# Turned heads written into the tiles of the output sums, a reordered output pair and later turns, in a two-layer hybrid encoder

## The chip, the cores and the metric

The kernel runs on one core of a Trainium2 chip. The core has TensorE (PE, matrix products), VectorE (DVE, elementwise), ScalarE (ACT, activations and casts), GpSimd (POOL, here small powers and the issue of DMAs) and SyncE (SP, here only the issue of DMAs). Each has its own queue of instructions, worked off in order; the transfers themselves run on DMA engines that all queues share. The metric is the device time of one execution in microseconds (us), as a median over runs; less is better.

## What is computed

Two layers of a streaming encoder on 512 tokens of width 2048, all in float32. One layer, cut to its core:

```python
h = rmsnorm(x, g_pre)
gq, gk, gv, gg, ga, aq, ak, av, ag = split_columns(h @ w_in)
log_a = log_sigmoid(ga @ w_alpha + b_alpha) / 16
o_gla = gla_chunk_causal(gq, gk, gv, log_a)        # 4 heads of 256 values
o_gla = rmsnorm(o_gla, g_gla) * silu(gg)
o_att = chunk_band_attention(aq, ak, av, rel_bias) # 8 heads of 128 values
o_att = rmsnorm(o_att, g_att) * silu(ag)
y = concatenate([o_gla, o_att]) @ w_out
x = x + rmsnorm(y, g_post)
```

What matters here is the end: the gated outputs of both head groups, concatenated to 2048 columns, are the left operand of the output projection.

## The kernel before

**Products.** A float32 value is split into a high part (a cast by ACT, L106 or L191) and a low part (a subtraction by DVE, L107 or L199), and a product takes three matmuls: high by high, high by low, low by high. Most products run in pairs of 512-column weight blocks by a scheme in the manner of Strassen (`fast_gemm`, L316): the operand is cut into token halves and halves of the 2048 rows, and seven products P1 to P7 of half size, on sums of operand quarters, take the place of eight. Each product runs over four chunks of 256 rows, so a pair is 28 jobs of 12 matmuls; "52" is P5 on the third chunk. The order of the 28 is written out: `PROD` (L132) for input pairs, `PROD_END` (L133) for output pairs. P1 and P2 and the last P4 use plain operands; P5, P6, P7 and P3 use the sums S1, S2, S3 and S4, which are made beforehand, written to DRAM and loaded again for each pair (`sa`). P2 of an output pair has accumulators of its own, two of the four auxiliary PSUM banks (L391). The weights' own sums are made by DVE as jobs come up (L185, L187).

**Jobs ahead.** `stream` (L206) lists all jobs in order. When a job has been issued, `ahead` (L240) issues the loads of weights (and of `sa`) up to five jobs ahead, casts up to four and low parts up to three. All these loads go through SP's queue, which is in order: a load that waits holds those behind it.

**Tasks and turns.** Side work is written as generators in the list `tasks`, and `pump` (L249) takes one step of the first of them; a `Pace` calls it after every job, three steps per job in the gate pair and the first output pair. Entries of `delayed` are run once they have been counted down by so many steps. The program so written is ordered once more per engine by a planner, which goes by modelled times and by when slots of tiles become free.

**The path into the output pair.** The last input pair is GG, the gate of the GLA heads (L1226). When one of its four results (P3, P7, P2, P4, in this order) is there, `gg_consume` (L1215) takes its SiLU (L1218) and multiplies two normalised heads by it (L1221). That gives two heads h for one token half p, 2 and 3 first, 0 and 1 with P2 and P4. Two and three steps later `turn_gla` (L1135) turns each: four transposes on PE (L1139), eviction with the gain by ACT (L1148) into `full_o`, a write of it to DRAM (`fg`, L1152, POOL's queue), and the split into the operand `og`. Chunk c of the output pair is GLA head c with attention heads 2c and 2c+1; the latter were turned during attention and lie in DRAM as `fa` (and, split, as `oa`). `output_sums` (L551) waits until both halves of head c are turned, loads the four quarters of the chunk from `fa` and `fg` into four tiles, and makes S1, S3, S2, S4 (L535 to L544), each split and written to DRAM (`oS`, L525, POOL's queue). The order of chunks is 2, 3, 0, 1.

**Tiles.** Tiles called `t2` come from a ring of eight; `full_o`, the SiLUs, the four quarters and many short results share it. Tiles named g0 to g17 are single slots reused in turn: in this part g9 and g10 have held GLA states and g12 and g13 the turned queries, and later the residual rows (L458, POOL's queue) come into g16, g17, g12, g13, g9 and g10. `residual_rows` (L1295) stands in the task list behind the sums.

After GG comes the first output pair, W01 (L1318), in both layers. In layer 0 the other half of the output follows as standard products (`std_gemm`), in layer 1 as a second fast pair, W23.

Of the kernel before, what the change touches and what calls it, by code (L numbers as in the profile page):

```python
# [8 lines left out]
F32R = mybir.dt.float32r  # L9
# [6 lines left out]
P = 128  # L16
L = 2
# [16 lines left out]
def hybrid_trunk(  # L34
# [34 lines left out]
    def slot(tag, shape, dtype=F32):  # L69
        return slots.tile([P] + shape, dtype, tag=tag, name=nm(tag))  # L70
# [4 lines left out]
    def t2(shape=(512,), dtype=F32):  # L75
        return tmp.tile([P] + list(shape), dtype, tag="t2", name=nm("t2"))
# [13 lines left out]
    def dram(shape, name):  # L90
        return dpool.tile(shape, F32, tag=name, name=name)
# [4 lines left out]
    so_d = [{(n, c): dram([P, 1024], f"o{n}{l}{c}") for n in ("S1", "S2", "S3", "S4") for c in range(4)} for l in range(L)]  # L96
    oa_d = [{(h, c): dram([P, 1024], f"oa{l}{h}{c}") for h in range(2) for c in range(4)} for l in range(L)]
    of_att = [[dram([P, 2, 512], f"fa{l}{c}") for c in range(4)] for l in range(L)]
    of_gla = [{(h, c): dram([P, 512], f"fg{l}{h}{c}") for h in range(2) for c in range(4)} for l in range(L)]
    fac_d = [dram([P, 1024], f"fac{l}") for l in range(L)]  # L100

    def flat(t):
# [26 lines left out]
    def order(text):  # L129
        return [("P" + z[0], int(z[1])) for z in text.split()]  # L130

    PROD = order("10 11 50 12 51 13 52 53 60 61 30 62 63 31 70 32 71 33 72 73 20 21 40 22 41 23 42 43")  # L132
    PROD_END = order("10 20 11 21 12 22 13 23 50 51 60 52 61 53 62 63 30 31 32 33 70 71 72 73 40 41 42 43")  # L133
    LEFT = {"P5": "S1", "P6": "S2", "P3": "S4", "P7": "S3", "P4": "A22"}
    last_cast = [None]

# [70 lines left out]
    for l in range(L):  # L207
        if l:
            stream += [Job(l, "std", c, AG0) for c in CO]
            stream += [Job(l, "std", c, AG0) for c in CO]  # L210
            stream += [Job(l, "std", c, AG1) for c in CO]
        else:
            stream += [Job(l, "std", c, b) for b in (AG0, AG1) for c in CO]
        for b0, b1 in PAIRS:
            pr = {}
            stream += [Job(l, k, c, b0, b1, pr) for k, c in PROD]
        for b0, b1 in (W01, W23) if l == L - 1 else (W01,):
            pr = {}
            stream += [Job(l, k, c, b0, b1, pr) for k, c in PROD_END]
        if l < L - 1:  # L220
            stream += [Job(l, "std", c, b) for half in range(2) for b in W23 for c in OL]

# [93 lines left out]
    def fast_gemm(l, pair, consume, rate=0.0, skip=0, feature_major=False, after=None, end=False, lag=0, ops=A):  # L316
# [5 lines left out]
        if end:  # L322
            target.update(P2="Z", P4="Y")
            starts.append("P4")
        prod = PROD_END if end else PROD
        pace = Pace(rate, skip)
        keep = {}

# [55 lines left out]
                                stop=(c == 3 and kk == 1 and m == 2), skip_group_check=True,  # L384
                            )

        if end:
            acc["Z"] = None
        for k, c in prod:
            if k == "P2" and end and c == 0:  # L390
                acc["Z"] = [aux(), aux()]  # L391
# [121 lines left out]
    def make_sums(dst, tags, parts, home={}, chunks=range(4)):  # L513
        stage = [0]

        def put(name, c, src):
            if (name, c) in home:
                op = A[name, c] = slot(home[name, c], [2, 512], F32R)
            else:
                tag = tags[stage[0] % len(tags)]  # L520
                op = rtile(tag, dtype=F32R) if tag == "H" else slot(tag, [2, 512], F32R)
                stage[0] += 1
            with tc.issue_after(last_cast[0]):
                split(op[:, 0, :], op[:, 1, :], src)
            nc.gpsimd.dma_start(dst[name, c], flat(op))  # L525
            written.add((id(dst), name, c))

        for c in chunks:
            got = parts(c)
            while got is None:  # L530
                yield
                got = parts(c)
            a11, a12, a21, a22 = got
            yield
            nc.vector.tensor_tensor(out=a22, in0=a21, in1=a22, op=ALU.subtract)  # L535
            put("S1", c, a22)
            yield
            nc.vector.tensor_tensor(out=a21, in0=a11, in1=a21, op=ALU.subtract)
            put("S3", c, a21)
            yield  # L540
            nc.vector.tensor_tensor(out=a22, in0=a22, in1=a11, op=ALU.subtract)
            put("S2", c, a22)
            yield
            nc.vector.tensor_tensor(out=a12, in0=a12, in1=a22, op=ALU.add)  # L544
            put("S4", c, a12)
            yield

    def token_sums(l):
        return make_sums(sa_d[l], STAGE, lambda c: (full[0, c][:, 0, :], full[0, c][:, 1, :], full[1, c][:, 0, :], full[1, c][:, 1, :]), HOME)

    def output_sums(l, chunks, ready, tags):  # L551
        def parts(c):
            if not ready(c):
                return None
            tiles = [t2() for _ in range(4)]
            for half in range(2):
                nc.sync.dma_start(
                    tiles[2 * half].rearrange("p (k n) -> p k n", k=2),
                    of_att[l][c][:, :, half * 256 : (half + 1) * 256],
                )  # L560
                nc.sync.dma_start(tiles[2 * half + 1], of_gla[l][half, c])
            return tiles

        return make_sums(so_d[l], tags, parts, chunks=chunks)

    def both(a, b):
        turn = 0
        live = [a, b]
        while live:
            turn += 1  # L570
            try:
                next(live[turn % len(live)])
                yield
            except StopIteration:
                live.remove(live[turn % len(live)])

    VT = ("g16", "g17", "g4", "g5", "g6", "g7", "g12", "g13")
    V, U = {}, {}
# [137 lines left out]
    def layer(l):  # L716
# [151 lines left out]
        class Head:  # L868
# [69 lines left out]
            def turn(self):  # L938
                c, kk = self.hd // 2, self.hd % 2
                if kk == 0:  # L940
                    turned[c] = [slot(tag, [2, 512], F32R) for tag in ("g16", "g17")]
                ps = aux()
                for t in range(NT):
                    nc.tensor.transpose(ps[:, t * P : (t + 1) * P], self.sg[:, t, :], ident)
                kt = 8 + self.hd
                f = t2()
                nc.scalar.activation(
                    f, ps, AF.Copy, scale=gcol[:, l * 2 * KT + KT + kt : l * 2 * KT + KT + kt + 1]
                )
                nc.gpsimd.dma_start(of_att[l][c][:, kk, :], f)  # L950
                ks = slice(kk * 256, (kk + 1) * 256)
                for half in range(2):
                    z = turned[c][half]
                    split(z[:, 0, ks], z[:, 1, ks], f[:, half * 256 : (half + 1) * 256])
                    if kk:
                        nc.gpsimd.dma_start(oa_d[l][half, c], flat(z))
# [96 lines left out]
        class Unit:  # L1053
# [63 lines left out]
            def evict(self):  # L1117
# [14 lines left out]
        OG = {(0, 2): "g14", (0, 3): "g15", (0, 0): "a120", (0, 1): "a121",  # L1132
              (1, 2): "g4", (1, 3): "g5", (1, 0): "g6", (1, 1): "g7"}

        def turn_gla(h, p):  # L1135
            ps = aux()
            for f in range(2):
                for tt in range(2):
                    nc.tensor.transpose(  # L1139
                        ps[:, f * 256 + tt * P : f * 256 + (tt + 1) * P],  # L1140
                        normed[h, p][:, tt, f * P : (f + 1) * P], ident,
                    )
            assert p or h >= 2 or ("P2", h) in passed
            op = slot(OG[p, h], [2, 512], F32R)
            full_o = t2()
            for f in range(2):
                kt = 2 * h + f
                nc.scalar.activation(  # L1148
                    full_o[:, f * 256 : (f + 1) * 256], ps[:, f * 256 : (f + 1) * 256], AF.Copy,
                    scale=gcol[:, l * 2 * KT + KT + kt : l * 2 * KT + KT + kt + 1],  # L1150
                )
            nc.gpsimd.dma_start(of_gla[l][p, h], full_o)  # L1152
            split(op[:, 0, :], op[:, 1, :], full_o)
            og[p, h] = op
            O[1, p, OC.index(h)] = op
# [41 lines left out]
                    op_att[0, i] = O[0, 0, OC.index(i)] = slot(f"a11{i}", [2, 512], F32R)  # L1197
                    nc.sync.dma_start(flat(op_att[0, i]), oa_d[l][0, i])

        def output_ready(c):  # L1200
            return 2 * c in heads_done and (0, c) in og and (1, c) in og

        def gv_consume(j, h, t, src, comb):
            if (j, h) not in gvh:
# [10 lines left out]
        def gg_consume(j, h, t, src, comb):  # L1215
            until(lambda: len(gla_done) == 4)
            sg = t2()
            nc.scalar.activation(sg, settled(src, comb), AF.Silu)  # L1218
            for i in range(2):
                dst = normed[2 * j + i, h][:, t, :]  # L1220
                nc.vector.tensor_tensor(out=dst, in0=dst, in1=sg[:, i * 256 : (i + 1) * 256], op=ALU.mult)  # L1221
                if t:
                    delayed.append([2 + i, lambda hd=2 * j + i: turn_gla(hd, h)])

        tasks.append(output_sums(l, OC, output_ready, ("g0", "g1", "g2", "g3")))
        fast_gemm(l, PAIRS[5], gg_consume, rate=3, after=fetch_operands)  # L1226
        A.clear()

# [64 lines left out]
        xs = []  # L1293

        def residual_rows():  # L1295
            while len(og) < 8:
                yield
            for half in range(2):
                xs.append(load_tokens(half, x_src, nc.gpsimd))
                yield  # L1300
# [89 lines left out]
```

## Time and profile before

| | |
|---|---|
| median of 3 runs | 1704.12 us (1702.9 to 1708.93) |
| the profiled execution | 1700.16 us, of which the span is 1698.4 |
| busy: PE, DVE, ACT, POOL | 1628.3, 1267.1, 912.5, 156.4 us |
| PE's mean granted clock | 0.982 of full speed |
| DMA | 461.85 MB, mean 272 GB/s |
| W01 of layer 0 | from 648.45 to 759.83 us |
| W01 of layer 1 | from 1495.31 to 1606.41 us |

Rows of a timeline have the start, the duration, the engine, the line, the operation and the tiles (out<-in); in brackets stands how long the engine was idle before it and what ended that. In these names mm and ax are PSUM banks, wh and wl the high and low parts of weights, sa a loaded sum, a and g operands in slots, t a t2 tile, bias and sg tiles that hold gated heads here. Rows of a stretch have its bounds, its length, each engine's busy time and instruction count, the granted clock, the busy share of the DMA engines and their rate. "PE mm L381 x336" is the chain's row for 336 matmuls in sequence. Rows with "SPq" or "POOLq" and KB are DMA issues of a stretch with their median time from issue to landing.

### The profile page before, as it was taken

The numbers are of one execution on the slowest core, as the hardware profiler recorded it, in microseconds if no ns is written. First come the engines' busy times: TensorE is split into PE (matmuls) and PEld (weight loads), VectorE is DVE, ScalarE is ACT, GpSimd is POOL, SyncE is SP. The second block draws the span as 40 slices with busy tenths as digits, with TensorE's granted clock in tenths as the row PEclk, the third lists the DMA queues.
The fourth block names the chain that finished last, engine by engine and source line by source line (L and its number), as shares of the span: only waits on it lengthen the run. The fifth ranks groups of instructions, "written<-read, shape, count | busy, mean of one in ns | idle before, by whom it ended". The sixth has DMA issues, their size and how long they took to land.

```text
span 1698.4 us, 24821 instructions
## 1 busy us (share of the span) xinstructions
PE 1628.3 (96%) x8986; PEld 1389.0 (82%) x8986; DVE 1267.1 (75%) x1647; ACT 912.5 (54%) x1502; POOL 156.4 (9%) x236
## 2 busy tenths in 40 slices
PE   9999999999999998599999999999999999975996
PEld 7888999998887776488888889999988877764884
DVE  5977777776778877685786667777767787786878
ACT  7554446566554555454774444465665555554552
POOL 0110000010100112100122000000101001121002
PEclk9999999999999998899999999999999999987998
DMA  8889695876868689896789486858668676998965
GB/s 339 270 332 320 215 311 173 306 252 211 275 234 290 223 311 345 298 338 209 239 288 400 153 324 207 306 179 307 237 225 282 230 290 205 330 333 310 357 220 201
DMA packets 141690, 461.85 MB, mean 272 GB/s; under 512 B 15412, under 2 KB 28084, under 8 KB 141568
## 3 DMA queue, kind: packets, MB, share of 16 engines
q1 hardware_dynamic: 120096, 384.97, 65.6%
q0 software_dynamic: 20896, 74.21, 11.5%
q8 instruction: 71, 1.16, 0.3%
q10 hardware_dynamic: 576, 1.08, 0.2%
q14 instruction: 51, 0.42, 0.1%
HBM read 392.29 MB, written 67.91 MB: 271 GB/s over the span
## 4 chain that ended last, share of the span: by engine, by line
PE 85%; DMA 6%; issue 5%; DVE 2%; POOL 1%; ACT 0%; SPq 0%; DVEq 0%; POOLq 0%; ACTq 0%
PE mm L381 42%; PE mm L371 18%; PE mm L302 15%; PE ax L919 2%; DMA oS<-g 1%; DMA sa<-oS 1%; DMA raw<-in_w_dram 1%; PE ax L1101 1%; PE ax L902 1%; PE ax L739 1%; PE ax L1073 1%; DVE wl L199 1%; DMA t<-fg 1%; PE ax L381 1%; DMA bias<-in_rel_dram 1%
## 5 line engine op out<-in xcount | busy, mean ns | idle before, releaser
L381 PE MATMUL mm<-wh,sa 128*128 128x512 f32 x1600 | 521.9, 397 | 35.9 <-DMA sa<-oS 21.0
L191 ACT CAST wh<-raw 128x1024 fp32r<-128x1024 f32 (+1 forms) x253 | 265.2, 1053 | 257.3 <-PE mm L381 81.6
L381 PEld LDWEIGHTS mm<-wh,sa 128*128 128x128 f32 x1600 | 302.2, 189 | 110.3 <-ACT g L106 31.2
L199 DVE TENSOR_TENSOR wl<-raw,wh 128x1024 fp32r<-128x1024 f32 (+1 forms) x253 | 307.5, 1219 | 113.3 <-PE mm L381 52.3
L191 ACT CAST wh<-H 128x1024 fp32r<-128x1024 f32 x240 | 251.6, 1051 | 224.3 <-PE mm L381 111.5
L199 DVE TENSOR_TENSOR wl<-H,wh 128x1024 fp32r<-128x1024 f32 x240 | 292.9, 1222 | 100.7 <-PE mm L381 44.4
L381 PE MATMUL mm<-wl,sa 128*128 128x512 f32 x800 | 314.9, 394 | 0.0
L371 PE MATMUL mm<-sa,wh 128*128 128x256 f32 x1280 | 236.5, 285 | 0.0
L381 PE MATMUL mm<-wh,a 128*128 128x512 f32 x608 | 200.9, 395 | 3.1 <-ACT wh L191 2.4
L371 PEld LDWEIGHTS mm<-sa,wh 128*128 128x128 f32 x1280 | 199.6, 192 | 0.1
L371 PE MATMUL mm<-sa,wl 128*128 128x256 f32 x640 | 181.6, 284 | 0.0
L381 PEld LDWEIGHTS mm<-wl,sa 128*128 128x128 f32 x800 | 151.4, 189 | 29.4
L185 DVE TENSOR_TENSOR H<-H,raw 128x1024 f32<-128x1024 f32 x132 | 160.6, 1220 | 11.1 <-DMA raw<-in_w_dram 9.8
L423 POOL TENSOR_TENSOR sm<-sm,mhalf 128x2 f32<-128x2 f32 (+2 forms) x42 | 57.7, 1375 | 851.1 <-DVE sm L929 449.0
L381 PEld LDWEIGHTS mm<-wh,a 128*128 128x128 f32 x608 | 113.2, 188 | 27.4 <-ACT wh L191 4.3
L381 PE MATMUL mm<-wl,a 128*128 128x512 f32 x304 | 119.9, 394 | 3.2 <-DVE wl L199 3.2
L371 PEld LDWEIGHTS mm<-sa,wl 128*128 128x128 f32 x640 | 122.6, 192 | 0.2
L187 DVE TENSOR_TENSOR raw<-H,raw 128x1024 f32<-128x1024 f32 x60 | 73.4, 1224 | 61.1 <-DMA raw<-in_w_dram 60.9
L371 PE MATMUL mm<-a,wh 128*128 128x256 f32 x512 | 95.1, 286 | 0.0
L302 PE MATMUL mm<-wh,a 128*128 128x512 f32 x288 | 91.8, 390 | 0.0
L333 ACT COPY ev<-mm 128x512 f32<-128x512 f32 x96 | 55.9, 583 | 58.0 <-PE mm L381 41.2
L302 PE MATMUL mm<-wh,g 128*128 128x512 f32 x240 | 82.0, 392 | 0.0
(229 smaller groups left out, 2381.8 us busy)
## 6 DMA issues: line engine op xcount, KB each, us to landing
raw<-in_w_dram SPq DMA_DIRECT2D x323, 512.0 KB, 4.9
sa<-S SPq DMA_DIRECT2D x184, 512.0 KB, 4.4
H<-in_w_dram SPq DMA_DIRECT2D x60, 512.0 KB, 5.4
sa<-A SPq DMA_DIRECT2D x48, 512.0 KB, 6.4
sa<-oS SPq DMA_DIRECT2D x48, 512.0 KB, 5.7
S<-g POOLq DMA_DIRECT2D x32, 512.0 KB, 9.3
oS<-g POOLq DMA_DIRECT2D x32, 512.0 KB, 6.5
oa<-g POOLq DMA_DIRECT2D x16, 512.0 KB, 6.9
```

The source lines that it names most:

```text
L185: nc.vector.tensor_tensor(out=h, in0=h, in1=r, op=ALU.add)
L187: nc.vector.tensor_tensor(out=r, in0=h, in1=r, op=ALU.subtract)
L191: last_cast[0] = nc.scalar.copy(self.wh[:, z, :], src[:, z, :]).ins
L199: nc.vector.tensor_tensor(out=self.wl[:, z, :], in0=self.src[:, z, :], in1=self.wh[:, z, :].bitcast(F32), op=ALU.subtract)
L302: nc.tensor.matmul(pss[o], a(part, kk, o) if callable(a) else a[:, part, t], rhs[:, kk, :], start=(i == 0 and kk == 0 and m == 0), stop=(i ...
L333: nc.scalar.copy(e, src[t])
L371: nc.tensor.matmul(dst, lhs[:, kk, f], a[:, part, tok], start=(fresh and kk == 0 and m == 0 and ft % 2 == 0), stop=(c == 3 and kk == 1 and ...
L381: nc.tensor.matmul(out_ps[t], a[:, part, tok], rhs[:, kk, :], start=(fresh and kk == 0 and m == 0), stop=(c == 3 and kk == 1 and m == 2), ...
L423: nc.gpsimd.tensor_tensor(out=out_r, in0=v, in1=mhalf[:, : v.shape[-1]], op=ALU.pow)
L739: nc.tensor.matmul(ps[0:96, half * 256 : (half + 1) * 256], wga[kt // 10][:, kt % 10, :], op[:, i, (kt % 2) * 256 : (kt % 2 + 1) * 256], s ...
L902: nc.tensor.transpose(ps[:, j * P : (j + 1) * P], self.prob[i][:, j * P : (j + 1) * P], ident)
L919: nc.tensor.matmul(o, self.pt[i][:, j * P : (j + 1) * P], av[hd // 4, j // 2][:, j % 2, (hd % 4) * P : (hd % 4 + 1) * P], start=(j == 0), ...
```

## The change

- The turned head no longer goes through DRAM. `turn_gla` evicts it into the tile that the sums read. These tiles are slots now, g9 and g10 for chunks 2 and 0, g12 and g13 for chunks 3 and 1, two quarters to a slot; they are taken at the first turn of a chunk, where the two loads of `fa` are issued too. `of_gla` and `output_sums` are gone; `make_sums` is called with the tiles.
- Turns wait 8 and 11 steps, not 2 and 3.
- W01 in both layers follows `PROD_OUT`: P2 of its last two chunks (those of heads 0 and 1) comes behind P6 of the first two, and P5 and P6 run chunk pair by chunk pair. The second output pair of layer 1 keeps `PROD_END`.
- In layer 1 the split of the second token half of the turned attention heads, which nothing reads there, is left out with its write.
- `residual_rows` has no guard of its own any more; `both`, which nothing called, and an assignment that had no use are gone.

```diff
@@ orders
     PROD_END = order("10 20 11 21 12 22 13 23 50 51 60 52 61 53 62 63 30 31 32 33 70 71 72 73 40 41 42 43")
+    PROD_OUT = order("10 20 11 21 12 13 50 51 60 61 22 23 52 53 62 63 30 31 32 33 70 71 72 73 40 41 42 43")
...
-        prod = PROD_END if end else PROD
+        prod = (PROD_OUT if b0 == NB_IN else PROD_END) if end else PROD
@@ sums
-    def output_sums(l, chunks, ready, tags):
-        def parts(c):
-            if not ready(c):
-                return None
-            tiles = [t2() for _ in range(4)]
-            for half in range(2):
-                nc.sync.dma_start(
-                    tiles[2 * half].rearrange("p (k n) -> p k n", k=2),
-                    of_att[l][c][:, :, half * 256 : (half + 1) * 256],
-                )
-                nc.sync.dma_start(tiles[2 * half + 1], of_gla[l][half, c])
-            return tiles
-
-        return make_sums(so_d[l], tags, parts, chunks=chunks)
@@ attention heads
-                    turned[c] = [slot(tag, [2, 512], F32R) for tag in ("g16", "g17")]
+                    turned[c] = [slot(tag, [2, 512], F32R) for tag in ("g16", "g17")[: 1 + (not last)]]
...
-                for half in range(2):
-                    z = turned[c][half]
+                for half, z in enumerate(turned[c]):
@@ layer
+        parts = {}
+
+        def out_parts(c):
+            if c not in parts:
+                halves = [slot(tag, [2, 512]) for tag in (("g9", "g10"), ("g12", "g13"))[c % 2]]
+                parts[c] = [halves[0][:, 0, :], halves[0][:, 1, :], halves[1][:, 0, :], halves[1][:, 1, :]]
+                for half in range(2):
+                    nc.sync.dma_start(
+                        parts[c][2 * half].rearrange("p (k n) -> p k n", k=2),
+                        of_att[l][c][:, :, half * 256 : (half + 1) * 256],
+                    )
+            return parts[c]
@@ turn_gla
-            full_o = t2()
+            full_o = out_parts(h)[2 * p + 1]
...
-            nc.gpsimd.dma_start(of_gla[l][p, h], full_o)
@@ readiness, steps, task
-        def output_ready(c):
-            return 2 * c in heads_done and (0, c) in og and (1, c) in og
+        def ready_parts(c):
+            return parts[c] if (0, c) in og and (1, c) in og else None
...
-                    delayed.append([2 + i, lambda hd=2 * j + i: turn_gla(hd, h)])
+                    delayed.append([8 + 3 * i, lambda hd=2 * j + i: turn_gla(hd, h)])
...
-        tasks.append(output_sums(l, OC, output_ready, ("g0", "g1", "g2", "g3")))
+        tasks.append(make_sums(so_d[l], ("g0", "g1", "g2", "g3"), ready_parts, chunks=OC))
@@ residual rows
         def residual_rows():
-            while len(og) < 8:
-                yield
             for half in range(2):
```

More of the change, by code (lines that the diff above doesn't have):

```diff
@@ L98, in hybrid_trunk @@
     of_att = [[dram([P, 2, 512], f"fa{l}{c}") for c in range(4)] for l in range(L)]
-    of_gla = [{(h, c): dram([P, 512], f"fg{l}{h}{c}") for h in range(2) for c in range(4)} for l in range(L)]
     fac_d = [dram([P, 1024], f"fac{l}") for l in range(L)]
@@ L218, in hybrid_trunk @@
             pr = {}
-            stream += [Job(l, k, c, b0, b1, pr) for k, c in PROD_END]
+            stream += [Job(l, k, c, b0, b1, pr) for k, c in (PROD_OUT if b0 == NB_IN else PROD_END)]
         if l < L - 1:
@@ L385, in matmuls @@
                             )
-        if end:
-            acc["Z"] = None
         for k, c in prod:
@@ L549, in token_sums @@
         return make_sums(sa_d[l], STAGE, lambda c: (full[0, c][:, 0, :], full[0, c][:, 1, :], full[1, c][:, 0, :], full[1, c][:, 1, :]), HOME)
-    def output_sums(l, chunks, ready, tags):
-        def parts(c):
-            if not ready(c):
-                return None
-            tiles = [t2() for _ in range(4)]
-            for half in range(2):
-                nc.sync.dma_start(
-                    tiles[2 * half].rearrange("p (k n) -> p k n", k=2),
-                    of_att[l][c][:, :, half * 256 : (half + 1) * 256],
-                )
-                nc.sync.dma_start(tiles[2 * half + 1], of_gla[l][half, c])
-            return tiles
-        return make_sums(so_d[l], tags, parts, chunks=chunks)
[L566 to L572, printed above, removed]
-                yield
-            except StopIteration:
-                live.remove(live[turn % len(live)])
     VT = ("g16", "g17", "g4", "g5", "g6", "g7", "g12", "g13")
@@ L1295, in residual_rows @@
         def residual_rows():
-            while len(og) < 8:
-                yield
             for half in range(2):
```

## The prediction

> **What bounds the kernel now.** I read the page first (shares, the chain), then a table of stretches, then the engines' timelines around the first output pair. The page says that TensorE is the bound:
>
> ```profile
> span 1698.4 us, 24821 instructions
> PE 1628.3 (96%) x8986; PEld 1389.0 (82%) x8986; DVE 1267.1 (75%) x1647; ACT 912.5 (54%) x1502; POOL 156.4 (9%) x236
> ...
> PE 85%; DMA 6%; issue 5%; DVE 2%; POOL 1%; ACT 0%; SPq 0%; DVEq 0%; POOLq 0%; ACTq 0%
> ```
>
> So only idle or slow PE time can be won, and the stretches say where it is. The rows are attention and the pairs after it in layer 0; the last eight products of the gate pair (GG); the first output pair (W01) of layers 0 and 1; and 30 us late in W01 of layer 1. The chain's row is a whole pair of 28 products that nothing disturbs.
>
> ```profile
> core 0: us, PE busy (x) PEld busy (x) DVE busy (x) ACT busy (x) POOL busy (x), PEclk, DMA share, GB/s
> 246.00:594.00 348.00, 347.53 (x2144) 302.60 (x2143) 265.16 (x397) 199.44 (x384) 28.01 (x30) 1.00 0.72 247
> 626.60:648.45 21.85, 21.85 (x104) 18.15 (x104) 16.77 (x22) 13.10 (x20) 3.18 (x6) 1.00 0.96 337
> 648.45:759.83 111.38, 85.08 (x355) 68.11 (x354) 85.65 (x103) 54.87 (x81) 12.96 (x25) 0.89 0.90 326
> 1495.31:1606.41 111.10, 85.26 (x357) 68.57 (x356) 86.25 (x103) 55.76 (x82) 12.96 (x25) 0.88 0.93 341
> 1580.00:1610.00 30.00, 30.00 (x134) 24.87 (x133) 26.10 (x29) 15.80 (x24) 0.00 (x0) 1.00 0.98 378
> ```
> ```profile
> 102.52 76.16 PE mm L381 x336
> ```
>
> A pair needs 76.2 us; W01 takes 111.4 and 111.1. Of the 35 us too much in each layer, 26 are idle (111.38 - 85.08), the rest a granted clock of 0.89. W01 begins at 648.45, where the left operand becomes a. PE's timeline shows two stalls per layer, at the same places:
>
> ```profile
> 648.45 0.39 PE L381 MATMUL mm<-wh,a 128*128 128x512 f32 x1
> ...
> 663.08 0.45 PE L1139 MATMUL ax<-cst,bias 128*128 128x128 f32 x1 [2.42 <-DVE bias L1221]
> 667.96 0.45 PE L1139 MATMUL ax<-cst,bias 128*128 128x128 f32 x1 [2.76 <-DVE bias L1221]
> 675.86 0.49 PE L1139 MATMUL ax<-cst,sg 128*128 128x128 f32 x3
> 709.36 0.77 PE L381 MATMUL mm<-wh,sa 128*128 128x512 f32 x1 [14.84 <-ACT g L106]
> 712.91 0.77 PE L381 MATMUL mm<-wh,sa 128*128 128x512 f32 x2
> 1509.81 0.45 PE L1139 MATMUL ax<-cst,bias 128*128 128x128 f32 x1 [2.44 <-DVE bias L1221]
> 1515.30 0.45 PE L1139 MATMUL ax<-cst,bias 128*128 128x128 f32 x1 [3.36 <-DVE bias L1221]
> 1555.04 0.77 PE L381 MATMUL mm<-wh,sa 128*128 128x512 f32 x1 [15.58 <-DMA sa<-oS]
> ```
>
> The first stall: turns stand ahead of P2 in PE's queue and wait for gated heads. The second: P5 of chunk 0 waits for S1. What made these late is in the queues of ACT, DVE and POOL and the chain:
>
> ```profile
> 637.56 0.81 PE L1139 MATMUL ax<-cst,g 128*128 128x128 f32 x6
> ```
> ```profile
> 642.53 0.69 DVE L338 TENSOR_TENSOR ev<-mm,ev 128x512 f32<-128x512 f32 x1 [1.04 <-PE mm L381]
> ...
> 654.29 0.68 DVE L535 TENSOR_TENSOR t<-t,t 128x512 f32<-128x512 f32 x1
> ```
> ```profile
> 646.89 0.82 ACT L1148 ACTIVATE t<-ax,gcol 128x256 f32<-128x256 f32 x2
> ...
> 660.30 1.15 ACT L1218 ACTIVATE t<-ev 128x512 f32<-128x512 f32 x2
> ...
> 666.54 0.62 ACT L1218 ACTIVATE t<-mm 128x512 f32<-128x512 f32 x1
> ...
> 692.86 0.83 ACT L1148 ACTIVATE t<-ax,gcol 128x256 f32<-128x256 f32 x2
> ```
> ```profile
> 670.20 0.43 DVE L1221 TENSOR_TENSOR sg<-sg,t 128x256 f32<-128x256 f32 x1
> ```
> ```profile
> 694.25 0.54 POOL L1152 DMA_DIRECT2D fg<-t  x1 [15.56 <-ACT t L1148]
> ```
> ```profile
> 648.79 5.09 DMA t<-fg
> ```
>
> Two turns' transposes are over by 638.4, but ACT evicts one of them only at 646.9; the last turn's are over by 676.4 and it is evicted at 692.9. P2's combined result is there at 643.2, its SiLU comes at 660.3; GG ended at 648.45, the SiLU of its last product starts at 666.5, the gating after it ends at 670.6. ACT is idle between, so these wait for what they write: a t2 tile. The ring has eight, and each chunk of the output sums holds four from the load of its parts to its last sum. On top comes the trip through DRAM: the last head leaves at 694.25; the first sum at 654.29 had waited for such a load, 5.09 us.
>
> **The change part by part.** The heads' trip goes: per layer 8 POOL issues and 8 SP issues and 16 transfers of 256 KB. Inside W01 of layer 0 that is 5 + 6 of them, 11 x 0.262 = 2.88 MB of 36.32:
>
> ```profile
> DMA packets 11880, 36.32 MB, mean 326 GB/s; under 512 B 1298, under 2 KB 2834, under 8 KB 11875
> ...
> oS<-g POOLq DMA_DIRECT2D x16, 512.0 KB, 6.7
> sa<-oS SPq DMA_DIRECT2D x16, 512.0 KB, 6.3
> ...
> t<-fg SPq DMA_DIRECT2D x6, 256.0 KB, 5.8
> fg<-t POOLq DMA_DIRECT2D x5, 256.0 KB, 7.3
> ```
> ```profile
> g<-in_x_dram POOLq DMA_DIRECT2D x5, 512.0 KB, 6.7
> ```
>
> The t2 tiles are free, so the SiLUs can follow their data: the last about 650 rather than 666.5. For it chunks 0 and 1 share g9, g10, g12, g13 with chunks 2 and 3 and wait for the last sum of these. The residual rows, of which five 512 KB loads had landed or started before W01 (the row above), now stand behind the sums on POOL: four to six of them, 2.1 to 3.1 MB, move into W01. W01 then carries 35.5 to 36.6 MB.
>
> Turns 6 + 2i places later: three places are a product of 76.2/28 = 2.72 us, so the last two turns stand behind the second and third product of W01, 5.4 and 8.2 us after GG, and no longer take their PSUM banks ahead of P2. If the gated heads are there by then, the first stall (5.2 and 5.8 us) costs nothing; if not, PE waits again.
>
> P2 of chunks 0 and 1 go behind P6 of chunks 2 and 3: P5 of chunk 0 is then the 13th product, not the 10th, 12 x 2.72 = 32.7 us after GG, at 681 plus what stalls remain. Its S1 needs the last turns (654), eviction, split and two sums (about 4 us at the 0.7 to 0.8 us of the rows above), POOL's write (6.7) and SP's load (6.3): 654 + 4 + 13 = 671, with 10 us to spare. P5 of chunk 2 comes as 7th instead of 9th, at 665; its turn was transposed at 638, so S1 can be there by 656. I let both second stalls go.
>
> The second half of turned in layer 1 goes: 8 casts and 8 subtractions of 0.4 us and four transfers, all inside attention, where PE is busy for 347.5 of 348 us in layer 0's like stretch: nothing. The guard taken from residual_rows is nothing too, since the task list reaches it only after the sums.
>
> What is late next? DVE is busy for 85.7 us of W01 and DMA for 0.90 of it; neither shrinks much, while PE's need is 76.2 plus some 2 of turns. DVE alone would allow 85.7. At the share that it has beside a full PE (26.10/30 = 0.87) it needs 98.4, or 92.6 if 5 us of the sums of chunks 2 and 3 move into the end of GG, where DVE has 21.85 - 16.77 = 5 us free. The DMA needs 35.5 to 36.6 MB at 378 GB/s, 94 to 97 us. W01 is bounded from below by 85.7 and from above by 111; I take 95, between the DVE's and the DMA's. That saves 111.4 - 95 = 16.4 and 111.1 - 95 = 16.1, together 32.5 us: 1700.16 (the profiled execution; its span is 1698.4) - 32.5 = 1667.7. The median of the runs stands 4.0 above that execution, so 1671.7; I say 1671.
>
> **The rivals.** (1) All stalls go and DVE is full throughout: W01 takes 85.7, saving 25.7 + 25.4: 1653. Against it: in no row above is DVE over 0.87.
>
> (2) The DMA sets the pace at the rate that it now has while busy, 326/0.90 = 362 GB/s: 36 MB take 99.5 us, saving 11.9 + 11.6: 1681. For it: share 0.96 before and 0.90 in W01; against it: 378 GB/s beside a full PE. The Trainium skill, "DMA: Bandwidth & Descriptors", section "Where 436 GB/s comes from", has the HBM side bind at about 358 GB/s per core; by it W01 would take, as an estimate, 36 MB / 358 = 100.6 us and the kernel 1683. The trace's 378 GB/s over 30 us does not agree with that as a ceiling.
>
> (3) The SiLUs were late because ACT's and DVE's orders are so, not for t2. Then the last gated heads come at 670.6 as now, and PE stands before their transposes from 654: 16 us and about 2 of slow clock per layer (709.36 to 712.91, 3.55 us for what takes about 2). The sums follow without a second stall. W01: 76.2 + 2 + 18 + the 6.3 us of small stalls (26.3 - 5.2 - 14.8): 102.5, saving 8.9 + 8.6: 1687.
>
> (4) It does nothing: S1 of chunk 0 is as late as the trip was, since DVE does its sums no earlier; within 8.5 us of 1704.
>
> (5) The other side: slower. SP's queue is in order. The load of of_att for chunk 1 now goes out with the first turn of that chunk, one product into W01 (651), and must wait until the sums of chunk 3 have read g12 and g13; weights stand behind it. Weights are asked for five products ahead, 13.6 us. In the trace the last subtraction of the second chunk's sums starts at 670.53:
>
> ```profile
> 670.53 0.70 DVE L544 TENSOR_TENSOR t<-t,t 128x512 f32<-128x512 f32 x1
> ```
>
> As now it would hold SP 20 us and PE 6; the gain outweighs that. It decides from a hold of 13.6 + 16 = 30 us on, sums that end after 681. At 690, say, PE loses 39 - 13.6 + 2 = 27 per layer against the 16 won: 11 lost twice, 1726.
>
> **How the numbers follow.** My forecast (1660 to 1677) has 0.40; (1) 0.10, (2) 0.15, (3) 0.13, (4) 0.07, (5) 0.15. Faster by over 0.5% (8.5 us, about what a measurement of this kernel can tell from none): the forecast and (1) to (3), 0.78; same 0.07; slower 0.15. The range runs from 1650, just below (1), to 1697, past (3) to the edge of no change; outside are (5) and some of (4).
>
> **What would show it.** Right: W01 about 95 us in both layers, no fg transfers, granted clock near 1, SiLUs within 3 us of their data, no wait over 3 us before L381 or the turns, DMA share there 0.95 or more. The forecast is wrong if PE waits for the gated heads under the turns (3), for raw or wh with SP standing before fa (5), for sa<-oS as now (4), or if W01 shrinks and the pair after it grows by the residual rows.

## The result, and the profile after

| | before | after |
|---|---|---|
| median of the runs | 1705.08 us (1702.9 to 1708.93) | 1678.62 us (1677.49 to 1680.4) |
| profiled execution (its span) | 1700.16 us (1698.4) | 1678.37 us (1676.5) |
| W01, layer 0 and layer 1 | 111.4 and 111.1 us | 101.6 and 98.9 us |

The ratio is 0.9843, with a 95% interval of 0.9823 to 0.9864: 1.6% faster, some 26 us. 1671 was forecast. In the profiled executions 21.8 us are gone, and the two W01 together give 9.8 + 12.2 = 22.0 of them; nothing outside W01 matters.

The first lines of the page of the changed kernel, and the stretches of it: W01 of both layers, and 15 us early in the first.

```profile
span 1676.5 us, 24715 instructions
PE 1622.6 (97%) x8986; PEld 1387.4 (83%) x8986; DVE 1261.3 (75%) x1639; ACT 908.0 (54%) x1494; POOL 142.5 (8%) x216
```
```profile
648.92:750.55 101.63, 83.37 (x355) 67.68 (x354) 79.57 (x96) 50.19 (x75) 11.88 (x23) 0.90 0.92 338
1485.23:1584.10 98.87, 83.42 (x357) 67.83 (x356) 79.33 (x95) 49.70 (x76) 11.88 (x23) 0.91 0.95 359
655.00:670.00 15.00, 15.00 (x74) 12.14 (x72) 15.00 (x21) 9.23 (x17) 4.89 (x9) 1.00 1.03 395
```

PE's idle time in W01 of layer 0 fell from 26.3 to 101.63 - 83.37 = 18.3 us. Its timeline says which stall went and which stayed (a row of turns, then all rows of layer 0 with a wait for a sum and the longest of layer 1):

```profile
664.87 0.60 PE L1123 MATMUL ax<-cst,sg 128*128 128x128 f32 x4
673.44 0.50 PE L381 MATMUL mm<-wh,sa 128*128 128x512 f32 x1 [3.42 <-DMA sa<-oS]
689.98 0.47 PE L381 MATMUL mm<-wh,sa 128*128 128x512 f32 x1 [1.01 <-DMA sa<-oS]
706.83 0.77 PE L381 MATMUL mm<-wh,sa 128*128 128x512 f32 x1 [13.82 <-DMA sa<-oS]
1540.15 0.77 PE L381 MATMUL mm<-wh,sa 128*128 128x512 f32 x1 [11.01 <-DMA sa<-oS]
```

The first stall is gone: no turn (L1123) has a bracket any more. The second is there still, 13.82 and 11.01 us, but it belongs to another product. The loads of sums on SP's queue tell which, since they come in the order of the products:

```profile
648.68 0.33 SPq L175 DMA_DIRECT2D sa<-oS  x1
662.00 0.90 SPq L175 DMA_DIRECT2D sa<-oS  x2
675.26 0.33 SPq L175 DMA_DIRECT2D sa<-oS  x1
684.00 0.33 SPq L175 DMA_DIRECT2D sa<-oS  x1
699.17 13.43 SPq L175 DMA_DIRECT2D sa<-oS  x5
```

Four loads serve P5 and P6 of chunks 2 and 3, the fifth (684.00) P5 of chunk 0, the sixth (699.17) P5 of chunk 1. So PE waits at 706.83 for S1 of chunk 1; S1 of chunk 0, for which it waited 14.84 us before, now costs 1.01. The writes agree: the sixth load follows the landing of the write issued at 688.72, and S2 of chunk 0, the next in the order of the products, had been written at 686.32 and had landed by 692.4. (Some expectations below call what PE waits for P6 and S2 of chunk 0. That was my misreading; the loads and writes correct it. Their forecasts of time don't depend on the name.)

Why is S1 of chunk 1 so late? ACT's queue first, the last SiLU (L1201) and the turns' evictions (L1132), then DVE's, the S1 sums (L533) and splits (L106), then POOL's:

```profile
650.67 0.59 ACT L1201 ACTIVATE t<-mm 128x512 f32<-128x512 f32 x1
...
659.68 0.83 ACT L1132 ACTIVATE g<-ax,gcol 128x256 f32<-128x256 f32 x2
...
670.70 0.87 ACT L1132 ACTIVATE g<-ax,gcol 128x256 f32<-128x256 f32 x2
```
```profile
669.87 0.68 DVE L533 TENSOR_TENSOR g<-g 128x512 f32<-128x512 f32 x1
...
677.71 1.22 DVE L199 TENSOR_TENSOR wl<-raw,wh 128x1024 fp32r<-128x1024 f32 x1 [3.68 <-issue]
...
679.46 0.68 DVE L106 TENSOR_TENSOR g<-g,g 128x512 fp32r<-128x512 f32 x1
680.06 0.68 DVE L533 TENSOR_TENSOR g<-g 128x512 f32<-128x512 f32 x1
...
685.34 1.89 DVE L106 TENSOR_TENSOR g<-g,g 128x512 fp32r<-128x512 f32 x3
```
```profile
680.44 0.53 POOL L523 DMA_DIRECT2D oS<-g  x1 [10.78 <-DVE g L106]
...
687.63 0.53 POOL L523 DMA_DIRECT2D oS<-g  x1 [0.22 <-issue]
688.19 0.54 POOL L456 DMA_DIRECT2D g<-in_x_dram  x1
688.72 0.53 POOL L523 DMA_DIRECT2D oS<-g  x1
```

The SiLUs follow their data, the last at 650.67 instead of 668.06. But the turns are now put off by the program: PE turns the second half of head 0 at 661.66, and its eviction is over by 663.2; those of head 1 are over by 671.6. The load of `fa` into the same slots lands at 668.7. S1 of chunk 0 is summed at 669.87 and its split ends only at 680.1, behind weights' subtractions in DVE's queue, of which one (677.71) had waited 3.68 us. Chunk 1's S1, summed at 680.06, goes into the same staging slot g0 and so waits for the write of chunk 0's (680.44, landed at 684.0); it is split by 687.2 and goes out at 688.72, behind another sum and a residual row. The chain then has its write and its load:

```profile
688.72 10.40 DMA oS<-g
699.17 7.53 DMA sa<-oS
706.83 41.23 PE mm L381 x170
```

### The profile page after: what moved, and what is told of

Read it like the earlier page. It is cut to its first block, busy times and chain, and to the rows that moved or that the text cites. A ratio compares the mean times of both kernels' runs of the same rounds, so it can differ in the third digit from the quotient of the medians.

```text
span 1676.5 us, 24715 instructions
## 1 busy us (share of the span) xinstructions
PE 1622.6 (97%) x8986; PEld 1387.4 (83%) x8986; DVE 1261.3 (75%) x1639; ACT 908.0 (54%) x1494; POOL 142.5 (8%) x216
## 3 DMA queue, kind: packets, MB, share of 16 engines
q0 software_dynamic: 19040, 67.92, 10.5%
## 4 chain that ended last, share of the span: by engine, by line
PE 85%; DMA 7%; issue 4%; DVE 2%; POOL 1%; ACT 0%; SPq 0%; DVEq 0%; POOLq 0%; ACTq 0%
PE mm L381 44%; PE mm L302 16%; PE mm L371 16%; DMA raw<-in_w_dram 3%; PE ax L891 2%; DMA sa<-oS 1%; DMA oS<-g 1%; DVE wl L199 1%; PE ax L1072 1%; PE ax L874 1%; PE ax L711 1%; PE ax L1044 1%; PE ax L381 1%; PE ax L855 1%; PE ax L854 1%
## 5 line engine op out<-in xcount | busy, mean ns | idle before, releaser
L185 DVE TENSOR_TENSOR H<-H,raw 128x1024 f32<-128x1024 f32 x132 | 160.4, 1219 | 6.1 <-DMA raw<-in_w_dram 4.8
```

Of the source, the lines that this page charges most:

```text
L185: nc.vector.tensor_tensor(out=h, in0=h, in1=r, op=ALU.add)
```

## The experiments

The change has three large parts: the heads' path (turned heads into the sums' tiles, no trip through DRAM), the order (`PROD_OUT`) and the delays of the turns (8 and 11 steps instead of 2 and 3). In what follows "load 6" is the time in layer 0 at which S1 of chunk 1 has landed in DRAM and is asked for again. Each kernel has its ratio to the kernel before with a 95% interval.

**The order undone.**

```diff
-    PROD_OUT = order("10 20 11 21 12 13 50 51 60 61 22 23 52 53 62 63 30 31 32 33 70 71 72 73 40 41 42 43")
+    PROD_OUT = PROD_END
```

> The changed kernel with the old order of products in the first output pair (P2 of chunks 0 and 1 in their old places, P5 of chunk 0 as tenth product). Theory A (the heads' path and the freed t2 tiles carry the gain; the order only gives the second stall 8 us of cover): the second stall grows by up to 8 us per layer, 1683 to 1696 us. Theory B (the order and the later turns carry the gain): 1698 us or more.

Measured: 1669.55 us (1668.44 to 1674.71), ratio 0.9787 [0.9757, 0.9817]; load 6 at 692.08, PE's wait 9.41 us. Neither theory allowed it: with the late turns, the new order costs 9 us. P5 of chunk 1 is the 14th product in both orders, so the order can't give it time; only P5 of chunk 0 is put back, by one place. The chain around the write that load 6 waits for, in this kernel:

```profile
688.51 3.52 DMA oS<-g
692.08 7.11 DMA sa<-oS
```

The write is issued at almost the same time as in the changed kernel (688.72), but takes 3.5 us and not 10.4. In layer 1 it is the same: 3.9 us against 11.6.

**The delays undone.**

```diff
-                    delayed.append([8 + 3 * i, lambda hd=2 * j + i: turn_gla(hd, h)])
+                    delayed.append([2 + i, lambda hd=2 * j + i: turn_gla(hd, h)])
```

> The changed kernel with turns 2 and 3 steps after the gating, as before. Theory A: the gated heads are early now, so PE waits a few us at most before the turns, and the sums start up to 5 us earlier: 1674 to 1686 us. Theory B: PE waits for the heads as before, 5 us or more per layer: 1688 to 1700 us.

Measured: 1661.61 us (1660.7 to 1662.28), ratio 0.9734 [0.9708, 0.976]. No theory had the later turns as a loss of this size; they cost 17 us. SP's loads of sums, PE's longest wait and the stretch of W01 of this kernel, as above for the changed one:

```profile
646.49 0.33 SPq L175 DMA_DIRECT2D sa<-oS  x1
662.55 0.85 SPq L175 DMA_DIRECT2D sa<-oS  x2
671.77 3.02 SPq L175 DMA_DIRECT2D sa<-oS  x2
689.37 0.84 SPq L175 DMA_DIRECT2D sa<-oS  x2
```
```profile
657.31 0.50 PE L381 MATMUL ax<-wh,g 128*128 128x512 f32 x1 [0.66 <-ACT g L1132]
...
696.35 0.77 PE L381 MATMUL mm<-wh,sa 128*128 128x512 f32 x1 [5.07 <-DMA sa<-oS]
```
```profile
647.50:740.68 93.18, 82.94 (x355) 66.40 (x354) 79.57 (x96) 49.45 (x75) 11.81 (x23) 0.96 0.98 367
```

Load 6 is 9.8 us earlier (1.4 of them because W01 begins earlier) and PE's wait 8.7 us shorter. The early turns, which the change moves out of the way of P2, cost P2 0.66 us here: with gated heads at hand there was nothing to move them out of. And W01 takes 93.2 us, with the DMA engines busy for 0.98 of it at 367 GB/s.

The last eviction is no earlier here than in the changed kernel (671.50 against 670.70), so the delays don't act through it. Chunk 0 is what comes earlier: its S1 is summed at 662.17 and not at 669.87. The write of chunk 1's S1, which follows in the same staging slot, is then issued at 681.04 and not at 688.72.

```profile
662.17 0.69 DVE L533 TENSOR_TENSOR g<-g 128x512 f32<-128x512 f32 x1
```
```profile
671.50 0.83 ACT L1132 ACTIVATE g<-ax,gcol 128x256 f32<-128x256 f32 x2
```

**Both undone: the path alone.** (The two diffs above together.)

> The changed heads' path alone: the changed kernel with both the old order of products and the old turns. The two parts cost time singly (undoing the order won 10 us, undoing the turns 18). If both costs have their own causes (the order brings four more weight sums of DVE ahead of the chunks' sums; the late turns start the sums later), they add: 1648 to 1656 us. If they share one cause, lateness of the last sums, undoing the order on top of the early turns gives nothing or loses the 8 us of cover per layer: 1660 to 1676 us.

Measured: 1665.54 us (1661.87 to 1667.82), ratio 0.9759 [0.9737, 0.978]; load 6 at 689.65. The path alone wins more than the whole change. The four kernels with the new path make a table (medians, us):

| | turns at 2 and 3 | turns at 8 and 11 | the delays cost |
|---|---|---|---|
| old order | 1665.5 | 1669.6 | 4.0 |
| new order | 1661.6 | 1678.6 | 17.0 |
| the order gives | -3.9 | +9.1 | |

The effects are not additive. The runs behind the -3.9 overlap, those behind the +9.1 do not.

**Order and delays without the path** (both put into the kernel before).

> The kernel before with the new order of the first output pair and the later turns alone; heads still go through DRAM and the sums' parts through t2. Theory A: the SiLUs stay 15 us late, so at most the 8 us of cover per layer are won: 1690 to 1705 us. Theory B: 1676 to 1686 us.

Measured: 1693.12 us (1691.5 to 1696.29), ratio 0.9921 [0.9893, 0.9949], as Theory A had it. With the old path the SiLUs are still late (the last at 659.7); there the two parts gain 12 to 14 us. What they are worth thus depends on the path.

**Halfway delays.**

```diff
-                    delayed.append([8 + 3 * i, lambda hd=2 * j + i: turn_gla(hd, h)])
+                    delayed.append([5 + 2 * i, lambda hd=2 * j + i: turn_gla(hd, h)])
```

> The changed kernel with its turns 5 and 7 steps after the gating, halfway between the 8 and 11 of the change (1678.6 us) and the 2 and 3 of before (1661.6 us). E (each step that a turn is put off reaches the sum S2 of chunk 0 and with it PE): the second turn is 4 of the 8 steps nearer, so about half of the 17 us: 1668 to 1672, with S2 of chunk 0 made between 676 and 679 us in layer 0 and PE's wait for it 7 to 11 us. F (there is slack, and only the last steps cost, where the last sums run into the full DVE): within 3 us of 1661.6, wait 4 to 6 us. G (any delay past the first product costs all): within 3 us of 1678.6.

Measured: 1669.81 us (1669.13 to 1670.26), ratio 0.9801 [0.9771, 0.9832]: the time is halfway, as E had it, with PE's wait a little below E's 7 to 11 us and S2 of chunk 0 a little early, at 675.27. SP's load 6 and PE's wait in this kernel:

```profile
693.14 11.81 SPq L175 DMA_DIRECT2D sa<-oS  x5
```
```profile
700.25 0.77 PE L381 MATMUL mm<-wh,sa 128*128 128x512 f32 x1 [6.69 <-DMA sa<-oS]
```

Across 2/3, 5/7 and 8/11 steps load 6 comes at 689.4, 693.1 and 699.2, and the time is 1661.6, 1669.8 and 1678.6. But the even steps are partly chance. W01 of layer 0 itself began at 647.50, 650.18 and 648.92. Counted from there, load 6 comes after 41.9, 43.0 and 50.3 us. In layer 1, counted from the start of W01 there (1475.36, 1477.99 and 1485.23), it comes after 41.3, 46.2 and 48.2 us. So the first half of the delay costs little in layer 0 and most in layer 1. That each step is handed on, as E had it, is not shown; with the old order the same eight steps cost only 4 us.

**The t2 ring freed, the trip kept:** the kernel before with the sums' quarters in slots, all else as it was.

```diff
-            tiles = [t2() for _ in range(4)]
+            halves = [slot(tag, [2, 512]) for tag in (("g9", "g10"), ("g12", "g13"))[c % 2]]
+            tiles = [z[:, i, :] for z in halves for i in range(2)]
```

> The kernel before with the sums' four parts in slots g9, g10, g12, g13 and not in t2; heads still go through DRAM, order and turns as before. Theory A, t2 was the cause: the SiLUs follow their data and the first stall goes, 1685 to 1698 us, with the second stall left. If the trip through DRAM was the cause instead: 1700 us or more, SiLUs as late as before.

Measured: 1702.0 us (1697.92 to 1705.49), ratio 0.9973 [0.9958, 0.9988]. The SiLUs (L1219 here) come earlier now, and no turn has a wait, but PE waits elsewhere (some of its rows, then DVE's S1 sums of chunks 0 and 1):

```profile
644.48 0.63 ACT L1219 ACTIVATE t<-ev 128x512 f32<-128x512 f32 x1 [0.31 <-DVE ev L338]
655.23 1.09 ACT L1219 ACTIVATE t<-mm 128x512 f32<-128x512 f32 x2
```
```profile
659.70 0.80 PE L381 MATMUL mm<-wl,a 128*128 128x512 f32 x1 [4.83 <-DVE wl L199]
687.66 0.76 PE L381 MATMUL mm<-wh,sa 128*128 128x512 f32 x1 [6.85 <-DMA sa<-oS]
...
716.87 0.77 PE L381 MATMUL mm<-wh,sa 128*128 128x512 f32 x1 [9.88 <-DMA sa<-oS]
```
```profile
689.58 1.29 DVE L535 TENSOR_TENSOR g<-g 128x512 f32<-128x512 f32 x2 [2.84 <-DMA g<-fg]
```

So the ring did make the SiLUs late, as the prediction said: those of the two combined results come at 643.5 and 644.5 instead of 660.3, the others at 655.2 instead of 666.5 and 668.1. But that alone is worth 0.3%. The rest of the path's 2.4% comes with what the path changes besides. The trip is the likely part: here S1 of chunk 0 is summed at 689.58, after a wait of 2.84 us for a head's load from DRAM. The earlier loads of `fa` and the missing guard of the residual rows came with the path too and were not tried apart from it.

**The second half of the turned attention heads put back in layer 1.**

```diff
-                    turned[c] = [slot(tag, [2, 512], F32R) for tag in ("g16", "g17")[: 1 + (not last)]]
+                    turned[c] = [slot(tag, [2, 512], F32R) for tag in ("g16", "g17")]
```

> The changed kernel with the second token half of the turned attention heads split and written again in layer 1. If that step is worth nothing, as predicted since PE is full there: within 3 us of the changed kernel, 1676 to 1682 us. If it is a part of the gain: 1684 us or more.

Measured: 1676.52 us (1674.71 to 1677.8), ratio 0.982 [0.9797, 0.9843]. Leaving that work out gains nothing that can be measured.

**The residual rows.** Two of them went to POOL's queue just ahead of the write of S1 of chunk 1. In the next kernel all are issued behind the last sum's write:

```diff
+    last_put = [None]
...
-            nc.gpsimd.dma_start(dst[name, c], flat(op))
+            last_put[0] = nc.gpsimd.dma_start(dst[name, c], flat(op)).ins
...
-                xs.append(load_tokens(half, x_src, nc.gpsimd))
+                with tc.issue_after(last_put[0]):
+                    xs.append(load_tokens(half, x_src, nc.gpsimd))
```

> The changed kernel with the residual rows issued behind the last write of a sum on GpSimd's queue. Theory C (the remaining stall comes from the rows that share queue and DMA with the writes of the last sums): the write that took 10.4 us takes about 7, the stalls of 13.8 and 11.0 us shrink by 4 to 6 us each, 1667 to 1672 us. Theory D (the last sums are made too late by DVE): at most 2 us per layer, 1675 to 1681 us.

Measured: 1674.45 us (1671.51 to 1677.12), ratio 0.9807 [0.9785, 0.9829]. Load 6 comes 8.6 us earlier, at 690.54: the write before it is issued at 683.44, and it takes 7.0 us, as Theory C had it. PE's wait for it shrinks from 13.82 to 5.98, but waits of 2.38 and 3.90 stand at other sums, and some 4 us are left of the gain. The time lies between the two theories' ranges. The same edit with early turns, with the new order and with the old:

> The changed kernel with the old turns (new order kept) and the residual rows behind the last write of a sum; without the latter it took 1661.6 us. Theory C: its stalls of 5.1 and 3.4 us go, 1652 to 1657 us. Theory D: within 3 us of 1661.

> The heads' path alone (old order, old turns) with the residual rows behind the last write of a sum. Theory C: 5 us or more below the same kernel without that. Theory D: within 3 us of it.

Measured: 1669.34 us (1668.6 to 1672.15), ratio 0.9786 [0.9767, 0.9805], and 1675.46 us (1673.4 to 1678.26), ratio 0.982 [0.98, 0.984]: 8 and 10 us slower than the same kernels with the rows where they were. All ten rows now start in one burst, in the last kernel between 695.9 and 706.4, just when the last sums are loaded; it has PE waits of 4.68 and 2.57 us there (POOL's queue at the start of the burst, then PE):

```profile
695.86 1.08 POOL L457 DMA_DIRECT2D g<-in_x_dram  x2
697.27 2.13 POOL L457 DMA_DIRECT2D g<-in_x_dram  x4 [0.33 <-issue]
```
```profile
703.39 0.76 PE L382 MATMUL mm<-wh,sa 128*128 128x512 f32 x1 [4.68 <-DMA sa<-oS]
719.21 0.47 PE L382 MATMUL mm<-wh,sa 128*128 128x512 f32 x1 [2.57 <-DMA sa<-oS]
```

Last, the rows on SP's queue behind W01's own loads, with new order and early turns:

```diff
+                last_load[0] = nc.sync.dma_start(tile_, src).ins
...
-                xs.append(load_tokens(half, x_src, nc.gpsimd))
+                with tc.issue_after(last_load[0]):
+                    xs.append(load_tokens(half, x_src, nc.sync))
...
-        tasks.append(residual_rows())
...
         fast_gemm(l, W01, out_consume(0), rate=3, end=True, ops=O)
+        tasks.append(residual_rows())
```

> The changed kernel with the old turns and all residual rows (4.2 MB per layer) loaded through SP's queue at the end of the first output pair. If the DMA's load in that pair is what is left (the pair takes 93 us there, with 36 MB): the pair takes 88 us or less, 1649 to 1655 us, unless the next pair pays for the rows. If DVE is what is left: 1658 to 1664 us.

Measured: 1660.7 us (1658.0 to 1663.16), ratio 0.9723 [0.9695, 0.9751], the same as with the rows on POOL (1661.61). The stretch of W01 and the chain behind it:

```profile
647.70:736.20 88.50, 81.25 (x354) 65.65 (x353) 78.96 (x95) 49.58 (x75) 7.48 (x15) 0.98 0.92 350
```
```profile
735.02 8.60 DMA g<-in_x_dram
743.68 7.77 DMA raw<-in_w_dram
```

W01 is 4.7 us shorter, at 88.5, and the DMA no longer full in it; the products after it then wait for weights that stand behind the rows. The bytes cost the same in either place.

**More staging for the sums:** new order and early turns, and two slots more than the four through which sums are split and written.

```diff
-        tasks.append(make_sums(so_d[l], ("g0", "g1", "g2", "g3"), ready_parts, chunks=OC))
+        tasks.append(make_sums(so_d[l], ("g0", "g1", "g2", "g3", "g8", "g11"), ready_parts, chunks=OC))
```

> The changed kernel with the old turns and six slots (g8 and g11 besides g0 to g3) in which the sums wait for their write. Theory: ACT's splits wait for the landing of a write four sums back, so the last sums come late by it; with six, S2 of chunk 0 and the writes of chunk 1 come 3 us or more earlier and the stalls of 5.1 and 3.4 us shrink: 1652 to 1658 us. Rival: DVE or the DMA is the limit, 1659 to 1664 us.

Measured: 1677.85 us (1675.89 to 1680.73), ratio 0.983 [0.9805, 0.9855]: 16 us slower than without the two slots. PE no longer waits for sums in W01 of layer 0, but for weights (its waits between 640 and 760 us):

```profile
PE mm L381 <- ACT wh L191: 5.3, 2, 3.7
PE mm L381 <- DVE wl L199: 3.5, 5, 1.9
PE ax L381 <- ACT wh L191: 2.4, 1, 2.4
```

PE's waits in this stretch come to 13.7 us, against 10.2 without the two slots, and the granted clock is lower for a while (0.90 and not 1.00 from the start of W01 to 665). The loss falls on both layers: from the start of W01 in layer 0 to that in layer 1 the kernel takes 6.8 us more, from there to its end 8.2. I didn't trace the rest. That the sums' splits now crowd the weights' casts in ACT's and DVE's queues is read from the kind of wait, not shown.

## Why the prediction was right and wrong

**The mechanism of the first stall was right.** The ring of t2 tiles made the SiLUs late (they are earlier with the ring freed alone). The rest of the path, the heads' trip above all as far as the traces tell, was the larger cost (path alone: 40 us; ring alone: 5). The first stall went. The SiLUs come within 3 us of their data. The second half of turned is worth nothing. Faster by over 0.5% was right.

**The step that failed is "I let both second stalls go".** The working behind it, S1 of chunk 0 at 654 + 4 + 13 = 671 with 10 us to spare, had three faults.
- It stopped at chunk 0. P5 of chunk 1 comes one place later, as the 14th in the old order and in the new, and its S1 goes through the same queues and the same slot after chunk 0's. The wait of 13.82 us is there.
- Its terms: the second half of head 0 was to be turned at 654, 5.4 us after GG; PE turned it at 661.66, 12.7 us after GG's end at 648.92. From there to the issue of the write stood 4 us; it was 680.44 - 661.66 = 18.8, of which 10.6 behind the sum. Write and load stood at 13; they took 3.5 + 6.0 for chunk 0 and 10.4 + 7.5 for chunk 1. PE had S1 of chunk 0 at 690, not 671.
- "The 13th product, not the 10th" is a wrong count: by the order written out, P5 of chunk 0 was the 12th before. The order gives it 2.7 us and not 8. The "8 us of cover" in the expectations rest on the same count.

**The later turns** had no price beyond that 654, and cost 17 us with the new order, 4 with the old. The heads were there, so PE lost nothing at the turns; it lost the time at the sums behind them.

**The size.** W01 was put at 95 us and took 101.6 and 98.9: 6.6 + 3.9 = 10.5 us more than forecast; by the forecast's own sum the profiled execution would have been at 1667.7 and was at 1678.4. The measured 1678.6 is in the range of 1650 to 1697, but just outside the 1660 to 1677 that the forecast gave itself. That it came so near is partly luck: the 95 us hold 19 us above PE's 76.2 that were meant for DVE and the DMA, and what filled them in layer 0 was 18.3 us of PE waiting for sums, which the forecast had let go. With the turns left early, W01 of layer 0 takes 93.2.

**The signs.** "In no row above is DVE over 0.87" spoke against a full DVE; in the changed kernel both PE and DVE were busy for 15.00 of 15 us from 655 on. DMA at 0.95 or more holds in layer 1 (0.95), not in layer 0 (0.92). W01 carried 34.31 and 35.54 MB, where 35.5 to 36.6 were reckoned. A granted clock near 1 and no wait over 3 us did not come: the clock was 0.90 and 0.91, and of the signs of being wrong, PE waiting for `sa<-oS`, that of (4), is there, for chunk 1 and not for chunk 0.

**The rivals.** (1) is out, since not all stalls went, and (4) by the 26 us gained. (2), the DMA as the pace, gave 1681, nearest to the result, but for another reason than happened: W01 ran at 338 and 359 GB/s with PE waiting for one sum. It comes close to being the bound once that wait is short: 0.98 busy at 367 GB/s over 93 us, and 88.5 us for W01 when the residual rows are moved out of it. The Trainium skill, "DMA: Bandwidth & Descriptors", section "Where 436 GB/s comes from", has the HBM side bind at about 358 GB/s per core; these 367 GB/s are above that, so it is no ceiling here. The Trainium skill, "HBM Reference", section "Specifications (TRN2)", says why: 358 is the share with both cores of a pair streaming, and a core alone gets well above it. With one core at work the trace agrees with the second page. (3) is refuted by the early SiLUs. (5) is refuted by SP's waits in the changed kernel from 620 to 760 us: the loads of `fa` (L1113) held the queue four times, 2.9 us at the longest, where 30 were needed:

```profile
SPq L1113 <- DVE g L106: 7.4, 4, 2.9
```

**What stays open.** Why the new order costs 9 us with late turns and nothing with early ones is only partly explained. DVE makes four of the weights' sums (L185) between 650 and 670 us in the changed kernel and two with the old order, ahead of the sums of chunk 0. But S1 of chunk 1 leaves no later by it: its write is issued at 688.72 and 688.51, and it is the write itself that takes 10.4 us against 3.5 (in layer 1, 11.6 against 3.9). In the 4 us ahead of it (layer 0) five other transfers of 512 KB were issued in the changed kernel, two with the old order; that these slow the write is likely, but no run tried it by itself. With the residual rows moved away, the write took 7.0. The best kernels found are the new path and order with early turns (1661.6 us) and that with the rows on SP (1660.7): ahead of both the kernel before and the changed one.

## What to carry to other kernels

When a change removes a wait, the moves that were there to live with that wait have to be priced again: with the trip through DRAM gone, delaying the turns no longer hid anything and, with the new order, cost 17 us of the 44 to be had. Follow a delay to the last consumer and not to the first: here chunk 0's sum was worked out and chunk 1's, one product later through the same staging slot, set the end. And a queue's side traffic is best left spread: gathered behind the urgent transfers, it cost 8 to 10 us where these were already early.

## What the runs showed of the hardware

- The write of a 512 KB sum took 3.5 us (issued at 680.44) and 10.4 us (at 688.72) within one stretch of the changed kernel; the DMA engines were busy for 0.95 of the first and 0.99 of the second, so their share hardly tells the two apart. In the 4 us ahead of the first, one other transfer of 512 KB was issued, ahead of the second five. The median in W01 is 7.7 us. The Trainium skill, "DMA: Bandwidth & Descriptors", section "Anatomy of one DMA — SWDGE (gpsimd) path", fits one such DMA with 2.0 us and its bytes at 436 GB/s, which is an estimate of 3.2 us for 512 KB: the write of 3.5 us comes near it, the slow one takes over three times that.
- PE and DVE can both be busy for all of 15 us with the clock at 1.00 and 395 GB/s of transfers beside them.
- After a long wait PE's clock is low for some microseconds: from 706.83 to 711.00, behind the 13.82 us, the granted clock is 0.50, and the first matmul takes 0.77 us, against 0.39 for one undisturbed. So a stall costs more than its idle time.
